# Sums kept in PSUM at the ends of two MLPs, rotary tables formed later, and a last pair of rows taken block by block, in a two-layer hybrid backbone

## The chip, the cores and the metric

The kernel runs on one core of a Trainium2 chip. The metric is device time in microseconds (us) of one execution, lower is better. The runs before the change give a median of 1191.76 us.

Names of engines in what follows: PE is the matrix engine, DVE the vector engine, ACT the scalar engine, POOL the gpsimd engine and SP the one that issues DMAs. PSUM is the accumulator memory that PE writes; ACT and DVE read and write it too.

## The reference, cut to what matters

A latent stream of 512 rows and a context stream of 256 rows, each row 1024 wide, go through two layers. Layer 0 mixes by pooling, layer 1 by attention (8 query heads, 2 key heads, width 128, rotary positions on latent rows), and each mixer is followed by a squared-ReLU MLP with 4096 hidden units. In layer 1 only the latent rows are needed behind the attention.

```python
def rms_norm(x, g):
    y = xf * lax.rsqrt(jnp.mean(xf * xf, axis=-1, keepdims=True) + EPS)
    return (y * g).astype(x.dtype)
def sq_relu_mlp(h, w_in, w_out):
    return jnp.square(jax.nn.relu(h @ w_in)) @ w_out
...
h_lat = modulate(rms_norm(x, g_mix_pre[i]), sh1, sc1)
...
x = x + gt1 * rms_norm(y_lat, g_mix_post[i])
m_lat = sq_relu_mlp(modulate(rms_norm(x, g_mlp_pre[i]), sh2, sc2), w_mlp_in[i], w_mlp_out[i])
x = x + gt2 * rms_norm(m_lat, g_mlp_post[i])
```

All is float32. Matrix products are made of three float32r products (high by high, high by low, low by high), so every operand is split into a rounded part "hi" (ACT) and a remainder "lo" (DVE).

## The kernel before, in words

Rows are handled in tiles of 128: latent tiles 0 to 3, context tiles 4 and 5. The stages follow one another: layer 0's mixer, layer 0's MLP (MLP0), keys, values and queries of layer 1 (K/V and Q), attention by head and tile, the attention's output product, layer 1's MLP (MLP1).

**The end of an MLP.** The hidden units are worked off in 16 groups of 256. The MLP's sums stand in `acc` in SBUF, one row of 1024 for each tile. `finish` does the last two groups: `out_mm` makes 24 matmuls for a tile into two PSUM tiles of 512 columns (three tiles of 512, 256 and 256 for the last tile of MLP1, `THIRDS`), and `out_ev` adds each to `acc` on DVE (L795). Then, per tile, `norm_a` squares the sum on ACT (L157, L158) and takes the power on POOL (L162), `norm_g` multiplies it by the gate on DVE (L321), `norm_r` adds it to the residual `xr` on DVE (L324), `norm_s` squares the new row (L157), and `norm_c` scales it into a row of `acc` (L496 on ACT or L498 on DVE). The tiles come in the order 4, 5, 0, 1, 2, 3. In the middle groups some tiles are "seeded": ACT copies `acc` into PSUM first (L775), PE adds on top, and ACT copies the sum back (L793).

**A pair of rows.** `modulated_pair` turns two finished rows: 16 transposes on PE (L349) into PSUM tiles `psx`, scale and shift of each 256-wide block (L357 on DVE or L360 on ACT, by a tuple), the hi split on ACT (L363 or L368) and the lo split on DVE (L364 or L369). In `fine` form the splits go by two blocks, else by four. The result feeds the next product on PE: K/V (L1028) behind MLP0, MLP1's first product (L566) behind the attention.

**Rotary tables.** `rope_load` fetches cosine and sine tables, `rope_tables` multiplies them by the head gains with six DVE instructions (L1013, L1017). `head_norm` reads them for latent tiles (L1053, L1056).

**The attention's output.** `attn_mm` makes the product (psy, L1269); `attn_ev` first multiplies by the gate on DVE (L321), then squares on ACT (L157). The last tile's second half comes as two pieces of 256. MLP1's first group is worked in two halves of 256 rows each, so that the first half can run while the last pair is prepared; its two hidden blocks f are worked one behind the other.

**What sets the order.** Each step is put at a hand-written time in `Steps`; a scheduler with a simulated timeline then orders every engine's instructions. Instructions marked `keep_in_program_order` stay in the order of the code. PSUM has two pools: `psA` (two tiles of two banks) and `psB` (four tiles of one bank: pso, psq, pk, psy and, for narrow pairs, psx).

Of the kernel before, what the change touches and what calls it, by code (L numbers as in the profile page):

```python
# [53 lines left out]
def backbone(ctx: ExitStack, tc, x, c, ctx_in, c_ctx, w_ada, b_ada, g_mix_pre, g_mix_post,  # L54
# [315 lines left out]

    gflat = gate.rearrange("p a n -> p (a n)")
# [121 lines left out]
    def norm_c(t, act, pool):  # L493
        r = rs[t][:, 0:1]
        if act:
            sc.activation(accv[:, t, :], xr[:, t, :], AF.Copy, scale=r)  # L496
        else:
            (gp if pool else ve).tensor_scalar(out=accv[:, t, :], in0=xr[:, t, :], scalar1=r, scalar2=None,  # L498
                                               op0=ALU.mult)
# [267 lines left out]
    def out_mm(i, parts, t, cols=HALVES):  # L767
        at_ = place_of[t] if i == 0 else t
        ts_ = slice(at_ * P, (at_ + 1) * P)
        seeded[t] = i == 0 and parts[0][0] > 0 and len(parts) == 1 and t in (1, 4) and stale[0] <= 0  # L770
        stale[0] -= 2
        pss = [psB.tile([P, 512], F32, tag="b", name="pso") for _ in cols]
        if seeded[t]:
            for (c0, w), ps in zip(cols, pss):
                sc.copy(ps, accv[:, t, c0:c0 + w])  # L775
# [11 lines left out]
    def out_ev(i, parts, t, cols=HALVES):  # L787
        for (c0, w), ps in zip(cols, pso[t]):
# [46 lines left out]
    def mlp1(inner, last):  # L835
# [38 lines left out]
        def squares(inner, q):  # L874
            for f in range(2):
                inner.part(len(inner.chunks) - 1, f)
# [133 lines left out]
    def rope_tables():  # L1010
        for w in (1, 0):
            g = grow[:, w, :]
            ve.tensor_tensor(out=tabs[:, w, 0], in0=tabs[:, w, 0],  # L1013
                             in1=g.unsqueeze(1).broadcast_to([P, NL, HD]), op=ALU.mult)
            for o in range(2):
                d = tabs[:, w, 1].rearrange("p t (h o d) -> p t h o d", o=2, d=32)[:, :, :, o, :]
                ve.tensor_tensor(out=d, in0=d, in1=swap(g, 1 - o).unsqueeze(1).broadcast_to([P, NL, 2, 32]),  # L1017
                                 op=ALU.mult)
# [49 lines left out]

    def norm_a(t, cols=HALVES):
        ss = sm_tile("ss")  # L1070
        for n, (c0, w) in enumerate(cols):
            mean_square(accv[:, t, c0:c0 + w], ss, n)
        rs[t] = rstd(ss, len(cols))

    def norm_g(t, pool=False, cols=HALVES):
        yg[t] = work_tile()
        for c0, w in cols:
            z = gated(t, yg[t], accv[:, t, c0:c0 + w], c0, c0 + w, pool)
            if cols == THIRDS:
                tc.keep_in_program_order(z)  # L1080
# [37 lines left out]
    def last0(st, n, t):  # L1118
        st.at([5.25, 10.45, 15.65, 20.85, 26.05, 31.25][n], norm_a, t)
        st.at([5.473, 10.6, 15.8, 21, 26.2, 31.4][n], norm_g, t, (False, False, False, False, False, False)[n])  # L1120
        st.at([8.8, 14, 19.2, 24.4, 29.6, 34.8][n], norm_r, t, (False, True, False, False, False, False)[n])
        st.at([10, 16.738, 20.4, 25.6, 30.8, 36][n], norm_s, t, (False, False, False, False, True, False)[n])
# [281 lines left out]
```

## Time and profile before

| | us |
|---|---|
| runs before: lowest, median, highest | 1187.81, 1191.76, 1194.09 |
| profiled execution, its own time | 1193.66 |
| its span | 1191.9 |
| PE busy | 1149.0 (96%) |
| DVE busy | 941.9 (79%) |
| ACT busy | 643.8 (54%) |
| POOL busy | 74.5 (6%) |

The profiled execution's own time is 1.76 us more than its span. Times in the views count from the span's start. A row of a timeline gives start, length, engine, line, operation, operands and count, and in brackets the idle time before it with what ended it; rows of one line that follow each other are merged, and a matmul's last piece overlaps the next row's start.

### The profile page before, as it was taken

Reading aid. Unit: us, or ns where it says so; the run is one execution under the profiler, and the core shown is the slowest. Engines: PE = TensorE matmul, PEld = TensorE weight load, DVE = VectorE, ACT = ScalarE, POOL = GpSimd, SP = SyncE. Lnnn points to the kernel's source line nnn. Section 1 sums busy time; section 2 is a strip of 40 time slices with the busy share of each in tenths; the row PEclk is TensorE's granted clock in tenths of the full one; section 3 lists DMA queues with packets and bytes.
Section 4 is the critical chain, followed back from the end, with each engine's and each line's share of the span. In section 5 each row is a group of like instructions: output and inputs, shape, how many; then the busy total and the mean of one; then the engine's idle time right before and its main releaser. Section 6 shows DMA issues by size and latency. Waiting matters only on the chain.

```text
span 1191.9 us, 15641 instructions
## 1 busy us (share of the span) xinstructions
PE 1149.0 (96%) x6026; PEld 993.8 (83%) x6026; DVE 941.9 (79%) x1521; ACT 643.8 (54%) x1141; POOL 74.5 (6%) x88
## 2 busy tenths in 40 slices
PE   6889999999999999999989989999899999999997
PEld 5568989899889888998867879998888888888886
DVE  5666686889989898998786589978677788778876
ACT  4676665445345534555775347872677346435523
POOL 1010000000000000000221232001000000000000
PEclk9899999999999999999998989999999999999999
DMA  9993222334434444344422111006244133314302
GB/s 339 389 319 121 72 75 102 118 130 142 157 126 142 141 140 144 107 155 138 166 71 79 64 36 37 1 6 207 108 140 145 39 135 123 113 47 142 106 31 111
DMA packets 92985, 147.88 MB, mean 124 GB/s; under 512 B 2752, under 2 KB 67824, under 8 KB 92912
## 3 DMA queue, kind: packets, MB, share of 16 engines
q1 hardware_dynamic: 92912, 146.90, 36.1%
q8 instruction: 47, 0.77, 0.3%
q14 instruction: 26, 0.21, 0.1%
HBM read 139.55 MB, written 7.34 MB: 123 GB/s over the span
## 4 chain that ended last, share of the span: by engine, by line
issue 45%; PE 43%; DVE 4%; ACT 3%; DMA 2%; POOL 2%; POOLq 0%; DVEq 0%; SPq 0%; ACTq 0%
PE psin L566 14%; PE pso L886 11%; PE psy L1269 3%; PE psq L1028 3%; PE po L1243 3%; PE pss L1204 2%; PE pspool L465 2%; PE pso L783 1%; PE pspt L1229 1%; ACT junk L157 1%; DMA raw<-in_w_ada 1%; POOL rs L162 1%; PE psada L229 1%; POOL rs L1037 1%; DVE work L321 1%
## 5 line engine op out<-in xcount | busy, mean ns | idle before, releaser
L783 PE MATMUL pso<-units,rb 128*128 128x512 f32 x1152 | 277.0, 392 | 0.0
L783 PEld LDWEIGHTS pso<-units,rb 128*128 128x128 f32 x1152 | 214.9, 188 | 41.7
L268 DVE SCALAR_TENSOR_TENSOR rows<-raw,cond,rows 128x256 f32<-128x256 f32 x280 | 123.0, 482 | 0.7
L795 DVE TENSOR_TENSOR acc<-acc,pso 128x512 f32<-128x512 f32 (+1 forms) x133 | 87.6, 675 | 34.5 <-PE pso L783 34.2
L566 PE MATMUL psin<-ra,rb 128*128 128x512 f32 (+2 forms) x384 | 103.2, 363 | 2.6 <-ACT ra L363 1.6
L162 POOL TENSOR_TENSOR rs<-ss,nhalf 128x1 f32<-128x1 f32 x42 | 27.1, 646 | 954.2 <-ACT ss L158 951.0
L886 PE MATMUL pso<-units,pairs 128*128 128x512 f32 x336 | 82.5, 389 | 0.0
L566 PEld LDWEIGHTS psin<-ra,rb 128*128 128x128 f32 x384 | 69.9, 192 | 13.1 <-ACT ra L535 1.9
L566 PE MATMUL psin<-ra 128*128 128x512 f32 x256 | 80.6, 389 | 0.0
L886 PEld LDWEIGHTS pso<-units,pairs 128*128 128x128 f32 x336 | 63.1, 188 | 13.1
L890 DVE TENSOR_TENSOR acc<-acc,pso 128x512 f32<-128x512 f32 x72 | 48.6, 681 | 29.0 <-PE pso L886 29.0
L677 PE MATMUL psin<-ra,units 128*128 128x384 f32 x336 | 65.7, 337 | 0.4 <-ACT psin L689 0.4
L677 PE MATMUL psin<-sums,units 128*128 128x384 f32 x336 | 63.6, 336 | 0.0
L677 PEld LDWEIGHTS psin<-ra,units 128*128 128x128 f32 x336 | 59.7, 188 | 3.1 <-ACT psin L689 0.5
L677 PEld LDWEIGHTS psin<-sums,units 128*128 128x128 f32 x336 | 59.0, 188 | 1.3
L566 PEld LDWEIGHTS psin<-ra 128*128 128x128 f32 x256 | 48.1, 188 | 10.0
L566 PE MATMUL psin<-rb 128*128 128x512 f32 (+1 forms) x144 | 53.5, 372 | 0.3 <-DVE rb L364 0.2
L1028 PE MATMUL psq<-units,ra 128*128 128x512 f32 x216 | 52.0, 393 | 0.0
L566 PE MATMUL psin<-rb,ra 128*128 128x512 f32 x128 | 49.8, 389 | 0.0
L122 DVE TENSOR_TENSOR units<-raw,units 128x1024 fp32r<-128x1024 f32 x34 | 41.2, 1216 | 9.7 <-ACT units L121 9.6
L1028 PEld LDWEIGHTS psq<-units,ra 128*128 128x128 f32 x216 | 40.1, 188 | 8.4 <-DVE ra L364 0.2
L793 ACT COPY acc<-pso 128x512 f32<-128x512 f32 x44 | 24.6, 586 | 35.8 <-PE pso L783 35.7
(271 smaller groups left out, 2379.8 us busy)
## 6 DMA issues: line engine op xcount, KB each, us to landing
raw<-in_w_ada SPq DMA_DIRECT2D x48, 1024.0 KB, 5.3
raw<-in_w_mlp_in SPq DMA_DIRECT2D x32, 1024.0 KB, 5.3
raw<-in_w_mlp_out SPq DMA_DIRECT2D x32, 1024.0 KB, 5.9
raw<-in_w_qkv SPq DMA_DIRECT2D x6, 1024.0 KB, 5.2
spill<-xr SPq DMA_DIRECT2D x10, 512.0 KB, 8.6
xr<-spill SPq DMA_DIRECT2D x10, 512.0 KB, 6.8
raw<-in_w_o SPq DMA_DIRECT2D x4, 1024.0 KB, 5.4
xr<-in_x SPq DMA_DIRECT2D x4, 512.0 KB, 4.9
```

The source lines that it names most:

```text
L122: ve.tensor_tensor(out=lo[:, z], in0=raw[:, z], in1=hi[:, z], op=ALU.subtract)):
L162: gp.tensor_tensor(out=r[:, 0:1], in0=ss[:, parts + 3:parts + 4], in1=nhalf[:, 0:1], op=ALU.pow)
L268: ve.scalar_tensor_tensor(out=r, in0=raw[:, k, :], scalar=cond[:, k, c:c + 1], in1=r, op0=ALU.mult, op1=ALU.add)
L566: te.matmul(ps[:, bank, o:o + ln], w[:, k, fs], a[:, k, t0:t0 + ln], start=(k == 0 and n == 0), stop=(k == KT - 1 and n == 2))
L677: te.matmul(bank, w[k], a[k], start=start and k == 0 and m == 0, stop=stop and k == 3 and m == 2, skip_group_check=True)
L783: te.matmul(pss[h][:, 0:cols[h][1]], a[:, f, ts_], w[:, f, cols[h][0]:sum(cols[h])], start=(n == 0 and not seeded[t]), stop=(n == len(seq) ...
L795: ve.tensor_tensor(out=d, in0=d, in1=ps[:, 0:w], op=ALU.add)
L886: te.matmul(ps, a, w, start=(m == 0), stop=(m == len(seq) - 1))
L890: ve.tensor_tensor(out=M[n][:, t], in0=M[n][:, t], in1=ps, op=ALU.add)
L1028: te.matmul(ps, a[:, k, sl], w[:, k % 4, :], start=(k == 0 and n == 0), stop=(k == KT - 1 and n == 2))
L1243: te.matmul(po[:, 0:256], v[:, kt, hs], p[:, kt, qs], start=(kt == 0 and n == 0), stop=(kt == NT - 1 and n == 2))
L1269: te.matmul(ps, a[:, k, sl], w[:, k % 4, o:o + width], start=(k == 0 and n == 0), stop=(k == KT - 1 and n == 2))
```

## The change

Four things change.

1. In `finish`, the sums of tiles 0 to 3 (MLP0) and of tiles 2 and 3 (MLP1) are seeded: ACT copies `acc` into the PSUM tile before the matmuls, PE adds on top, and `out_ev` does nothing for them. `norm_a` and `norm_g` then read the sum from PSUM (`summed`). Tiles 4 and 5 (MLP0), 0 and 1 (MLP1) stay as they were.
2. The steps of MLP0's last tiles get earlier times; tile 3's row is scaled on DVE; `rope_tables` moves from time 18.4 to 38.5, and its six instructions are kept in program order.
3. The attention's last pair gets a function of its own, `last_pair`: transposes of row tile 2 first and then those of row tile 3, all in `psB`, scale, hi and lo split block by block (256 wide). Tile 3's residual and squares are done in halves and its row is scaled half on DVE and half on ACT; tile 2's row is scaled on DVE; tile 3 is squared before it is gated.
4. MLP1's first group works the first four k blocks for both hidden blocks f before it goes on.

```diff
+    def last_pair(t, i, s, hi, lo, on_act):
+        works, sh = [accv[:, t + u, :] for u in range(2)], (SH1, SH2)[s] * KT
+        pss = [psB.tile([P, 2, 256], F32, tag="b", name="psx") for _ in range(KT // 2)]
+        for u in range(2):
+            for k in range(KT):
+                te.transpose(pss[k // 2][:, k % 2, u * P:(u + 1) * P], works[u][:, k * P:(k + 1) * P], ident)
+        for k in range(KT):
...
+            if on_act[k]:
+                sc.activation(h, src, AF.Identity, scale=sa, bias=b)
+            else:
+                ve.tensor_scalar(out=h, in0=src, scalar1=sa, scalar2=b, op0=ALU.mult, op1=ALU.add)
+            sc.copy(hi[:, k, z], h)
+            ve.tensor_tensor(out=lo[:, k, z], in0=h, in1=hi[:, k, z], op=ALU.subtract)
...
-    def norm_c(t, act, pool):
+    def norm_c(t, act, pool, half=False):
         r = rs[t][:, 0:1]
+        if half:
+            ve.tensor_scalar(out=accv[:, t, 0:512], in0=xr[:, t, 0:512], scalar1=r, scalar2=None, op0=ALU.mult)
+            sc.activation(accv[:, t, 512:D], xr[:, t, 512:D], AF.Copy, scale=r)
+            return
...
-        seeded[t] = i == 0 and parts[0][0] > 0 and len(parts) == 1 and t in (1, 4) and stale[0] <= 0
+        if len(parts) > 1:
+            seeded[t] = t not in ((4, 5), (0, 1))[i]
+        else:
+            seeded[t] = i == 0 and parts[0][0] > 0 and t in (1, 4) and stale[0] <= 0
...
     def out_ev(i, parts, t, cols=HALVES):
+        if len(parts) > 1 and seeded[t]:
+            return
...
+            n = len(inner.chunks) - 1
+            early_ = range(KT // 2 if n else 0)
+            for k in early_:
+                for f in range(2):
+                    inner.part(n, f, (k,))
             for f in range(2):
-                inner.part(len(inner.chunks) - 1, f)
+                inner.part(n, f, range(len(early_), KT))
...
+    def summed(t, cols):
+        return [ps[:, 0:w] if seeded[t] else accv[:, t, c0:c0 + w] for (c0, w), ps in zip(cols, pso[t])]
+
     def norm_a(t, cols=HALVES):
         ss = sm_tile("ss")
-        for n, (c0, w) in enumerate(cols):
-            mean_square(accv[:, t, c0:c0 + w], ss, n)
+        for n, src in enumerate(summed(t, cols)):
+            mean_square(src, ss, n)
...
-        st.at([10, 16.738, 20.4, 25.6, 30.8, 36][n], norm_s, t, (False, False, False, False, True, False)[n])
+        st.at([10, 16.738, 20.4, 25.6, 28.5, 30.4][n], norm_s, t, (False, False, False, False, True, False)[n])
...
-            st.at(18.4, rope_tables)
+            st.at(38.5, rope_tables)
...
+            last = (ch, t) == (1, NL - 1)
+            if last:
+                mean_square(ps, ss1[t], ch + n)
             gated(t, y1[:, t, :], ps, c0, c0 + width)
-            mean_square(ps, ss1[t], ch + n)
+            if not last:
+                mean_square(ps, ss1[t], ch + n)
...
+                if t == 3:
+                    at(47.4, last_pair, 2, 1, 1, h1H, h1L, (False, False, True, True, False, False, True, True))
```

How the order moves is read at three places; each row is a line, an operation, its output and inputs, the size and the count. The line numbers behind the change are those of the changed file.

On PE, where K/V begins behind MLP0's last product: `psx` are the transposes of the pairs (L349 in both files), `psq` the K/V products (L1028 before, L1061 now) and `pk` the transposed keys. Before:

```order
L1028 MATMUL psq<-units,ra 128x512 x10
L1028 MATMUL psq<-rb,ra 128x512 x2
L1028 MATMUL psq<-units,ra 128x512 x12
L1028 MATMUL psq<-rb,ra 128x512 x12
L1028 MATMUL psq<-units,ra 128x512 x12
L349 MATMUL psx<-ident,acc 128x128 x16
L1101 MATMUL pk<-ident,xr 128x128 x2
```

Now:

```order
L1061 MATMUL psq<-units,ra 128x512 x18
L349 MATMUL psx<-ident,acc 128x128
L1061 MATMUL psq<-rb,ra 128x512 x6
L349 MATMUL psx<-ident,acc 128x128
L1061 MATMUL psq<-rb,ra 128x512 x6
L1061 MATMUL psq<-units,ra 128x512 x8
L349 MATMUL psx<-ident,acc 128x128 x14
L1061 MATMUL psq<-units,ra 128x512 x4
L1135 MATMUL pk<-ident,xr 128x128 x2
```

Before, all 72 products of tiles 4, 5 and 0 stand ahead of the last pair's 16 transposes; now the pair's first transpose stands behind 48 of them, and its last 14 behind 68.

On ACT, in MLP0's last product: L157 and L158 square a sum (`acc`, now `pso`) or a row (`xr`), L496 (now L517) scales a finished row, L799 is the seeding copy. Before:

```order
L157 ACTIVATE junk,ss<-acc 128x512
L496 ACTIVATE acc<-xr,rs 128x1024
L158 ACTIVATE ss<-ss,phase 128x1
L157 ACTIVATE junk,ss<-acc 128x512
L158 ACTIVATE ss<-ss 128x1
L157 ACTIVATE junk,ss<-xr 128x1024
L158 ACTIVATE ss<-ss,phase 128x1
```

Now:

```order
L157 ACTIVATE junk,ss<-pso 128x512
L517 ACTIVATE acc<-xr,rs 128x1024
L799 COPY pso<-acc 128x512
L158 ACTIVATE ss<-ss 128x1
L799 COPY pso<-acc 128x512
L157 ACTIVATE junk,ss<-xr 128x1024
L158 ACTIVATE ss<-ss,phase 128x1
```

The two seeding copies of tile 2 stand behind the scaled row of tile 4, which waits for POOL; PE's matmuls of tile 2 wait for these copies. Tile 3's copies stand likewise behind the scaled row of tile 0.

On DVE, at the attention's last pair: L369 is the lo split of the pair of tiles 0 and 1, L324 the residual of tile 3, L498 (now L519) and L513 scale rows, L357 and L384 scale and shift transposed blocks, L364 and L386 are lo splits. Before:

```order
L369 TENSOR_TENSOR rb<-acc,ra 128x4x256
L324 SCALAR_TENSOR_TENSOR xr<-acc,rs,xr 128x1024
L498 TENSOR_SCALAR acc<-xr,rs 128x1024
L357 TENSOR_SCALAR acc<-psx,avec_97,mods_93 128x256 x4
L364 TENSOR_TENSOR rb<-acc,ra 128x2x256 x4
L132 TENSOR_TENSOR ra<-raw,ra 128x2048
```

Now:

```order
L324 SCALAR_TENSOR_TENSOR xr<-acc,rs,xr 128x512
L369 TENSOR_TENSOR rb<-acc,ra 128x4x256
L324 SCALAR_TENSOR_TENSOR xr<-acc,rs,xr 128x512
L513 TENSOR_SCALAR acc<-xr,rs 128x512
L384 TENSOR_SCALAR acc<-psx,avec_97,mods_93 128x256 x4
L386 TENSOR_TENSOR rb<-acc,ra 128x256 x8
L132 TENSOR_TENSOR ra<-raw,ra 128x2048
```

The residual is halved around the lo split of the earlier pair, half of the row's scaling is left to ACT, and four wide lo splits become eight narrow ones.

40 lines of the change are left out of this document (21 added, 19 removed).

## The prediction

> **What bounds the kernel now.** I read the page's first part, then the table of windows around the three places that the change touches, then the timeline of each engine there. The busy times of the engines:
>
> ```profile
> PE 1149.0 (96%) x6026; PEld 993.8 (83%) x6026; DVE 941.9 (79%) x1521; ACT 643.8 (54%) x1141; POOL 74.5 (6%) x88
> ```
>
> PE is busy in 1149.0 of 1191.9 us. Since the change takes no matmul away, all that can be won is PE's idle time, the time it ran at half clock, and what lies behind its last matmul; work taken from DVE or ACT counts only where PE waits for them. The windows at these places (columns: window, length, busy PE, PEld, DVE, ACT, POOL, granted clock, DMA share, GB/s):
>
> ```profile
> 567.00:603.00 36.00, 36.00 (x170) 29.97 (x169) 26.12 (x34) 25.51 (x55) 11.66 (x11) 1.00 0.34 128
> 599.30:621.20 21.90, 20.74 (x96) 15.95 (x95) 20.00 (x33) 16.64 (x41) 7.12 (x7) 1.00 0.31 97
> 622.51:625.93 3.42, 1.24 (x7) 0.80 (x5) 1.57 (x2) 2.30 (x8) 0.54 (x1) 1.00 0.00 0
> 625.93:632.76 6.83, 5.30 (x21) 4.92 (x22) 4.54 (x12) 4.91 (x15) 2.75 (x7) 0.50 0.01 2
> 640.00:700.00 60.00, 59.56 (x277) 49.55 (x277) 40.91 (x69) 27.12 (x93) 15.98 (x23) 1.00 0.22 71
> 851.21:854.62 3.41, 1.65 (x14) 1.45 (x14) 0.75 (x1) 1.32 (x4) 0.55 (x1) 1.00 0.39 154
> 854.62:858.03 3.41, 1.55 (x12) 1.11 (x11) 2.82 (x6) 3.41 (x7) 0.00 (x0) 1.00 0.01 2
> 858.03:861.45 3.42, 3.42 (x17) 3.42 (x18) 2.56 (x4) 3.41 (x4) 0.00 (x0) 0.50 0.00 0
> 860.50:890.80 30.30, 30.30 (x150) 25.87 (x149) 26.41 (x26) 21.07 (x30) 0.00 (x0) 0.98 0.40 139
> ```
>
> MLP0's end (567 to 603) has PE busy throughout. Behind it K/V loses time in two ways, by waits and by a clock of 0.50 from 625.93 to 632.76. The same pair of losses stands at the attention's last pair (851 to 861). So the change can gain at these two places and at the end of the program, and lose in 567 to 603, where nothing is to be won.
>
> **The change, term A: MLP0's end to K/V.** PE's timeline there:
>
> ```profile
> 595.45 1.69 PE L349 MATMUL psx<-ident,acc 128*128 128x128 f32 x14
> 596.89 6.16 PE L783 MATMUL pso<-units,rb 128*128 128x512 f32 x26
> ...
> 617.64 3.16 PE L1028 MATMUL psq<-rb,ra 128*128 128x512 f32 x10 [0.81 <-DVE ra L364]
> 620.63 2.90 PE L1028 MATMUL psq<-units,ra 128*128 128x512 f32 x12
> 623.37 0.38 PE L349 MATMUL psx<-ident,acc 128*128 128x128 f32 x2
> 627.46 3.25 PE L349 MATMUL psx<-ident,acc 128*128 128x128 f32 x14 [3.71 <-ACT acc L496]
> ```
>
> From the starts, a K/V product costs (623.37 - 620.63)/12 = 0.228 and a transpose (596.89 - 595.45)/14 = 0.103. MLP0's last product starts ahead of 602.9. The 72 products and 32 transposes behind it need 72 x 0.228 + 32 x 0.103 = 19.7, so without a wait they would end at 622.6. They end at 627.46 + 3.25 = 630.7: 8.1 lost. The greatest part is the wait of 3.71 for tile 3's scaled row (L496), the next the half clock, at which the 14 transposes take 3.25 in place of 1.45 (1.8 lost). The rest of the half-clock stretch to 632.76 costs (632.76 - 630.7)/2 = 1.0 more. So 9.1 is the most that can be had.
>
> What ACT does there, and tile 3's chain:
>
> ```profile
> 598.97 1.06 ACT L157 ACTIVATE junk<-xr 128x1024 bf16<-128x1024 f32 x1 [1.59 <-DVE xr L324]
> 619.45 0.62 ACT L157 ACTIVATE junk<-acc 128x512 bf16<-128x512 f32 x1
> 622.37 1.28 DVE L324 SCALAR_TENSOR_TENSOR xr<-work,rs,xr 128x1024 f32<-128x1024 f32 x1 [0.46 <-POOL rs L162]
> 626.27 1.14 ACT L496 ACTIVATE acc<-xr,rs 128x1024 f32<-128x1024 f32 x1
> ```
>
> Tile 3's sum is squared only at 619.45, 17 us behind its product. Now the squares read PSUM and their steps come earlier. By the order, what ACT has from the square at 598.97 to tile 2's scaled row is: seven casts of 512 (0.52 from start to start), four blocks of L360 (0.47), six squares of 512 with their reads (0.62), seven L158 (0.2), two squares of 1024 and two scaled rows (1.05 each): 14.9 together. Without idle time the row is ready at 613.9; I add half of the idle time that ACT had there before (599.3 to 621.2: 21.90 - 16.64 = 5.26), since L360 still waits for transposes: 616.5. PE, with 48 products and 16 transposes behind it, is there at 602.9 + 12.6 = 615.5. The next products take a hi (a cast, 617.1) and a lo of 0.7 on DVE (617.8). Tile 3's row follows: by the order its last L158 has two casts, two L360, a cast and a small cast ahead of it, about 3.5 us, then POOL 0.55 and DVE's scaling 0.75, so 621.4 against 627.4 before. PE, with 18 products and 2 transposes behind 617.8, reaches its 14 transposes at 622.1: the long wait is gone. 22 products and 16 transposes from 617.8 take 6.7, end 624.5; with 1.5 for short waits, as much as before, 626.0. Gain 630.7 - 626.0 = 4.7, and 1.0 for the half clock behind it.
>
> Against it stand the rotary tables:
>
> ```profile
> 610.00 0.68 DVE L1013 TENSOR_TENSOR acc<-acc,grow 128x512 f32<-128x512 f32 x1
> 610.60 0.74 DVE L1017 TENSOR_TENSOR acc<-acc,grow 128x256 f32<-128x256 f32 x2
> ```
>
> Twice this is 2.8 us, formerly in DVE's gaps, now between tile 3's row and the last pair's scaling (L357) on DVE. K/V products of the last pair wait for these blocks, and the first rotary use follows. Bounds 0 and 2.8; I take 0.7, a quarter, as ACT takes some of the eight blocks and products of the earlier pairs stand between. **A = -4.7 - 1.0 + 0.7 = -5.0**. Bounds: -0.3 (ACT as idle as before, 2.6 later, and the tables at 2.8) and -7.5 (ACT with no idle time, so that PE's own 615.5 counts, 1.0 more, and no short waits, 1.5 more).
>
> The seeds are costed at nothing. The relevant rows:
>
> ```profile
> L775 ACT COPY pso<-acc 128x512 f32<-128x512 f32 x44 | 25.6, 587 | 27.0 <-DVE acc L795 26.9
> 579.81 4.69 POOL L132 TENSOR_TENSOR rb<-raw,rb 128x2048 fp32r<-128x2048 f32 x1 [1.25 <-ACT rb L129]
> 586.91 1.14 ACT L496 ACTIVATE acc<-xr,rs 128x1024 f32<-128x1024 f32 x1
> 595.61 1.14 ACT L496 ACTIVATE acc<-xr,rs 128x1024 f32<-128x1024 f32 x1
> ```
>
> Thirteen copies at 0.587 (three of them shorter) are 7.2 us on ACT, eight of them in 567 to 603, where ACT is busy 25.51 of 36; 25.5 + 4.7 = 30.2 still fits. But PE waits for each. A tile's 24 products take 24 x 0.228 = 5.5: back from 602.9 PE wants tile 3's seed at 597.4, and, with 16 transposes more, tile 2's at 590.2. Tile 2's copies follow tile 4's row (586.91 + 1.14 = 588.05): 588.6 and 589.4. Tile 3's follow tile 0's row (596.75 at its old time): 597.3, and the second at 598.0, wanted at 600.1. The order has a tile's first half ahead of its second, so it fits by 1.6 us at tile 2 and by 0.1 at tile 3; the old time of tile 0's row is a late one, as two squares that waited for L795 stood ahead of it. If the cover fails, the rival below gives the price. The thirteen evictions that DVE loses (0.675 each, 8.8 us) free time where PE didn't wait for DVE, save in term C.
>
> **Term B: the attention's last pair.**
>
> ```profile
> 847.96 0.38 ACT L157 ACTIVATE junk<-psy 128x256 bf16<-128x256 f32 x1
> 849.75 1.29 DVE L324 SCALAR_TENSOR_TENSOR xr<-acc,rs,xr 128x1024 f32<-128x1024 f32 x1 [0.44 <-POOL rs L162]
> 853.21 0.75 DVE L498 TENSOR_SCALAR acc<-xr,rs 128x1024 f32<-128x1024 f32 x1 [2.17 <-POOL rs L162]
> 854.02 1.53 PE L349 MATMUL psx<-ident,acc 128*128 128x128 f32 x12 [1.76 <-DVE acc L498]
> 857.19 0.50 PE L566 MATMUL psin<-ra,rb 128*128 128x256 f32 x2 [1.64 <-ACT ra L363]
> 857.91 0.49 PE L566 MATMUL psin<-rb 128*128 128x256 f32 x1 [0.22 <-DVE rb L364]
> 857.17 2.50 DVE L364 TENSOR_TENSOR rb<-acc,ra 128x512 fp32r<-128x512 f32 x4
> 860.52 2.29 DVE L132 TENSOR_TENSOR ra<-raw,ra 128x2048 fp32r<-128x2048 f32 x1 [0.86 <-ACT ra L129]
> 865.01 0.40 PE L566 MATMUL psin<-ra 128*128 128x512 f32 x1
> ```
>
> Tile 3's row is ready at 853.96. The square of its last piece no longer waits for the gate (before, at 847.96, it stood behind a 1024 cast), the residual of 1.29 and the square overlap by halves, and the scaling of 0.75 is shared by two engines: I take 1.7 for all three, row at 852.3. Tile 2's transposes are then done, so eight remain (0.8), and scale, hi and lo of one block, by half of the 512-wide rows some 0.5, 0.35 and 0.4, with the starts between: first product at 854.3, the first with a lo at 855.0 (before 857.2 and 857.9). 48 narrow products at 0.121 end at 860.9, where before they end at 865.0 with 1.7 lost to the half clock. That is 4.1 earlier. The next weights limit it: their lo (L132) ends at 862.8 before and moves only with DVE, whose pieces grow from four of 0.64 to eight of 0.42, so I put the small end at 0.9, the wait ahead of L132 that ACT's cast made; and DVE is busy 26.41 of the 30.30 us behind. The weights of the first groups are, however, there for another k, so I stand nearer the upper end: **B = -3.0**, bounds -0.9 and -4.1.
>
> On the clock: the windows 851.21 to 854.62 and 854.62 to 858.03 had PE busy 1.65 and 1.55 of 3.41, neither of them idle, and the next one got 0.50. By that row a half-busy window is enough. Now the first window would hold about 2.1 busy and the second about 3, which lie above it, so full clock is assumed. [...]
>
> **Term C: the end.**
>
> ```profile
> 1185.00 0.42 DVE L795 TENSOR_TENSOR acc<-acc,pso 128x256 f32<-128x256 f32 x1 [0.55 <-PE pso L783]
> 1185.84 0.40 ACT L157 ACTIVATE junk<-acc 128x256 bf16<-128x256 f32 x1
> 1186.80 0.55 POOL L162 TENSOR_TENSOR rs<-ss,nhalf 128x1 f32<-128x1 f32 x1 [4.72 <-ACT ss L158]
> 1187.38 1.42 DVE L324 SCALAR_TENSOR_TENSOR xr<-work,rs,xr 128x512 f32<-128x512 f32 x2 [0.69 <-POOL rs L162]
> ```
>
> The last piece no longer passes L795 (0.42). Its square began at 1185.84, another 0.42 behind the eviction's end, as it stood behind the square of the piece before; that one is rid of its eviction too. **C = -0.8**, bounds -0.4 (ACT's queue stays) and -0.84 (all of both). The power on POOL and L324 stay as they are, and the seeds of MLP1 stand well ahead of them.
>
> MLP1's interleaved f blocks only make room for B and are counted there.
>
> **The sum.** -5.0 - 3.0 - 0.8 = -8.8. Against the profiled execution's own 1193.66 that is 1184.9; it lies 1.9 above the median of the runs, so on 1191.76 the forecast is **1183.0**.
>
> **The rivals.**
>
> *Seeds late (slower).* ACT is in order: if tile 4's row waits for POOL beyond 589.6, or tile 0's beyond 596.8, PE stops with nothing else to run. The 4.69 us on POOL at 579.81 is such a stretch, and the powers stand behind it in POOL's queue. With 3 us at each of two tiles and a half clock for 10.2 us (three windows, 5.1 lost) it costs 11.1, and with ACT late A's gain is gone: -3.8 + 11.1 = +7.3, 1199.1. Against it: powers now start earlier, by the evictions left out.
>
> *A is absorbed (same).* If Q and what follows start by DVE or POOL, a K/V that ends 5 us sooner only waits later; -3.8, 1188.0. For it: the rotary tables are pushed towards Q. Against it: PE is busy 59.56 of 60 in 640 to 700, DVE 40.91.
>
> *B stays behind the weights (small gain).* B = -0.9: sum -6.7, 1185.1. For it: L132 waited for ACT's cast of these weights before (0.86 ahead of 860.52), and that cast stays behind the pair's eight hi splits.
>
> *It does not do what it says:* the order shows the evictions gone and rows earlier; only waits can undo it. 1191.8.
>
> **How the numbers follow.** About 0.5% (6 us) is what a measurement of this kernel can tell from no change: faster is under 1185.8. Forecast 0.56, B behind the weights 0.12, A absorbed 0.20, seeds late 0.09, nothing gained 0.03. Faster takes 0.54 of the first and 0.07 of the second: 0.61; slower is 0.09; the rest 0.30. Low: all upper bounds are -7.5 - 4.1 - 0.8 = -12.4, 1179.4, less 1.4 for the scatter of the runs, 1178.0. High: the small ends give -0.3 - 0.9 - 0.4 = -1.6, 1190.2, plus 0.8 for the same scatter, 1191.0; the late seeds and no gain lie outside.
>
> **What would show it.** Right: PE's wait of 3.71 ahead of the 14 transposes is gone and 625.93 to 632.76 is at full clock; L807's matmuls (the former L783) have no idle time before tiles 2 and 3; the first wide product of MLP1 some 3 us earlier from the pair's start; L795 absent behind the last matmul. Wrong: idle time of PE ended by the seeding copy, a DVE that is still the releaser of K/V's products behind the rotary tables, or a Q stage that starts no earlier.

## The result and the profile after

| | before | changed |
|---|---|---|
| median of the runs, us (4 each) | 1192.69 | 1183.24 |
| lowest and highest | 1187.81, 1194.09 | 1180.60, 1184.12 |
| span of the profiled execution | 1191.9 | 1178.8 |

The ratio of the times is 0.9924, 95% interval 0.9903 to 0.9946: faster by 9.4 us, where 8.8 was forecast (1183.0).

PE, DVE, ACT and POOL in the changed kernel, and the windows at the two places (window, length, busy PE, PEld, DVE, ACT, POOL, granted clock, DMA share, GB/s):

```profile
PE 1145.2 (97%) x6026; PEld 989.4 (84%) x6026; DVE 935.4 (79%) x1515; ACT 648.6 (55%) x1160; POOL 75.9 (6%) x88
```

```profile
566.50:602.20 35.70, 35.67 (x166) 29.37 (x164) 24.55 (x29) 28.94 (x63) 12.53 (x10) 1.00 0.34 123
602.20:622.80 20.60, 20.53 (x106) 16.79 (x106) 16.05 (x27) 17.13 (x46) 8.53 (x12) 1.00 0.31 102
624.98:631.80 6.82, 6.82 (x32) 5.46 (x31) 6.19 (x14) 4.38 (x14) 0.89 (x2) 1.00 0.00 0
842.70:846.15 3.45, 2.20 (x13) 1.36 (x11) 2.90 (x8) 3.45 (x10) 0.00 (x0) 1.00 0.00 0
846.15:849.56 3.41, 3.41 (x17) 3.41 (x18) 2.21 (x6) 3.41 (x5) 0.00 (x0) 0.51 0.01 2
```

Through MLP0's last product (566 to 602) PE is still not idle (35.67 of 35.70), so no seed is late; through K/V (602 to 623) it is hardly idle either (20.53 of 20.60), and the half clock is gone there. At the last pair a half clock of 3.41 us stays. The first seeding copies of tiles 2 and 3, and the matmuls that need them:

```profile
586.99 0.58 ACT L799 COPY pso<-acc 128x512 f32<-128x512 f32 x1
589.35 5.73 PE L807 MATMUL pso<-units,rb 128*128 128x512 f32 x24
...
595.17 0.59 ACT L799 COPY pso<-acc 128x512 f32<-128x512 f32 x1
596.36 5.70 PE L807 MATMUL pso<-units,rb 128*128 128x512 f32 x24
```

The copies end at 587.57 and 595.76, 1.8 and 0.6 us ahead of PE.

PE's timeline of the changed kernel where the 3.71 stood, and the row that it had waited for on DVE, with ACT's row of tile 2:

```profile
618.36 2.00 PE L1061 MATMUL psq<-units,ra 128*128 128x512 f32 x8
620.20 1.69 PE L349 MATMUL psx<-ident,acc 128*128 128x128 f32 x14
621.65 1.17 PE L1061 MATMUL psq<-units,ra 128*128 128x512 f32 x4
...
612.94 1.15 ACT L517 ACTIVATE acc<-xr,rs 128x1024 f32<-128x1024 f32 x1
...
617.85 0.75 DVE L519 TENSOR_SCALAR acc<-xr,rs 128x1024 f32<-128x1024 f32 x1
```

Tile 3's row is there at 618.6, 1.6 ahead of its transposes; the 14 take 1.69 where they took 3.25.

At the last pair, PE and the end of the program:

```profile
841.99 1.09 PE L376 MATMUL psx<-ident,acc 128*128 128x128 f32 x8
844.05 0.50 PE L587 MATMUL psin<-ra,rb 128*128 128x256 f32 x2 [0.97 <-ACT ra L385]
844.76 0.39 PE L587 MATMUL psin<-rb 128*128 128x256 f32 x1 [0.20 <-DVE rb L386]
852.70 0.50 PE L587 MATMUL psin<-ra 128*128 128x512 f32 x1
...
1171.87 0.88 PE L807 MATMUL pso<-units 128*128 128x256 f32 x6
1172.79 0.38 ACT L157 ACTIVATE junk<-pso 128x256 bf16<-128x256 f32 x1 [0.63 <-PE pso L807]
1174.32 1.41 DVE L324 SCALAR_TENSOR_TENSOR xr<-work,rs,xr 128x512 f32<-128x512 f32 x2 [0.60 <-POOL rs L162]
```

One wait of 0.97 is left of 1.76 and 1.64. At the end the square starts straight behind PE (1172.79), with no eviction between, and the last residual 1.57 behind PE's end at 1172.75; before it was 1187.38 - 1184.96 = 2.42 (its last six matmuls: 1184.08, 0.88).

**Where the 13.1 us between the two profiled spans lie.** PE has 6026 matmuls in both, so the start of the one with the same number can be compared at any place at which the order is alike again. To the 3,100th (MLP0's last product) the changed kernel is 1.0 us ahead: scatter of the beginning, where nothing differs. So a time on the changed trace's clock is 1.0 less than the same moment on the clock of before, up to there. From there to the 3,400th (the first queries) it gains 7.85: term A. To the 3,700th (start of the attention) 1.4 more: behind the same wait (3.50 and 3.51) the half clock lasts 10.24 us in the one trace (704.43 to 714.67, granted 0.50) and 6.83 in the other (696.01 to 702.84, granted 0.50). From the 4,480th to the 4,600th (the last pair) 1.95: term B. Behind the last matmul 0.85: term C. A, B and C make 10.65. The same numbers are given for the experiments below, against the changed kernel's trace: "A +1.1" says that this stretch was 1.1 us longer there.

### The profile page after: what moved, and what is told of

Read it like the earlier page. It is cut to its first block, busy times and chain, and to the rows that moved or that the text cites. A ratio compares the mean times of both kernels' runs of the same rounds, so it can differ in the third digit from the quotient of the medians.

```text
span 1178.8 us, 15653 instructions
## 1 busy us (share of the span) xinstructions
PE 1145.2 (97%) x6026; PEld 989.4 (84%) x6026; DVE 935.4 (79%) x1515; ACT 648.6 (55%) x1160; POOL 75.9 (6%) x88
## 4 chain that ended last, share of the span: by engine, by line
PE 82%; issue 5%; ACT 5%; DVE 4%; POOL 2%; DMA 1%; POOLq 0%; DVEq 0%; SPq 0%; ACTq 0%
PE pso L807 22%; PE psin L698 18%; PE psin L587 17%; PE pso L917 11%; PE psy L1303 4%; PE po L1277 3%; PE pss L1238 2%; PE pspool L482 1%; ACT junk L157 1%; PE pspt L1263 1%; POOL rs L1070 1%; PE psada L229 1%; POOL rs L162 1%; DVE work L1086 1%; ACT ss L158 1%
## 5 line engine op out<-in xcount | busy, mean ns | idle before, releaser
L821 DVE TENSOR_TENSOR acc<-acc,pso 128x512 f32<-128x512 f32 x120 | 79.6, 679 | 32.3 <-PE pso L807 32.2
L917 PEld LDWEIGHTS pso<-units,pairs 128*128 128x128 f32 x336 | 63.1, 188 | 13.1
L921 DVE TENSOR_TENSOR acc<-acc,pso 128x512 f32<-128x512 f32 x72 | 48.7, 682 | 28.5 <-PE pso L917 28.5
L1061 PE MATMUL psq<-units,ra 128*128 128x512 f32 x216 | 52.1, 392 | 0.0
L799 ACT COPY pso<-acc 128x512 f32<-128x512 f32 (+1 forms) x57 | 32.6, 578 | 26.9 <-DVE acc L821 26.7
L1061 PEld LDWEIGHTS psq<-units,ra 128*128 128x128 f32 x216 | 40.1, 188 | 8.2
```

What stands on the lines that cost most here:

```text
L821: ve.tensor_tensor(out=d, in0=d, in1=ps[:, 0:w], op=ALU.add)
L917: te.matmul(ps, a, w, start=(m == 0), stop=(m == len(seq) - 1))
L921: ve.tensor_tensor(out=M[n][:, t], in0=M[n][:, t], in1=ps, op=ALU.add)
L1061: te.matmul(ps, a[:, k, sl], w[:, k % 4, :], start=(k == 0 and n == 0), stop=(k == KT - 1 and n == 2))
```

## The experiments

Eleven more kernels were run, eight of them the changed kernel with a part of the change taken back or altered; ratios are to the kernel before. Runs of one kernel differ by 0.3% and more, so a difference under 3 us is read in the traces: by the ratios, only the two runs at 0.9974 and 0.9967 can be told from the changed kernel's 0.9924.

**No seeds in MLP0.**

```diff
-            seeded[t] = t not in ((4, 5), (0, 1))[i]
+            seeded[t] = i == 1 and t not in (0, 1)
```

> The changed kernel, but MLP0's tiles 0 to 3 are not seeded: the evictions L821 (formerly L795) are back for them and the squares read acc; all step times stay as changed. In the traces of before and after, the K/V products behind MLP0 end 7.9 us earlier once the different start of the two executions (1.0) is taken off. Theory (the forecast's reason: tile 3's row comes early because its squares no longer stand behind evictions and late steps, and both the seeds and the times matter): eviction puts tile 3's squares some 2 us later, its row at about 620.5 in place of 618.6 on the after trace's clock, so K/V ends 0.5 to 2 us later than after, and 1 more where a half clock comes back; total +1 to +3 us against after. Rival S (the seeds carry the gain): the wait of 3 to 4 us ahead of the last 14 transposes returns, +7 to +8. Rival T (the step times alone carry it, seeds are worth nothing): 0 within 0.5 us in the trace.

Ratio 0.9974 (0.9954 to 0.9993). The earlier step times put tile 3's squares and gate ahead of its own evictions, so they read the sum without the last product; the time is that of such a kernel. A +6.7. DVE's rows show what it did: tile 3's two evictions are done only behind its scaled row.

```profile
622.19 0.74 DVE L519 TENSOR_SCALAR acc<-xr,rs 128x1024 f32<-128x1024 f32 x1
623.53 0.42 DVE L1077 TENSOR_TENSOR work<-psq,rs 128x256 f32<-128x256 f32 x1 [0.60 <-POOL rs L1070]
623.88 1.27 DVE L821 TENSOR_TENSOR acc<-acc,pso 128x512 f32<-128x512 f32 x2
```

The two PSUM tiles stay taken until 625. It doesn't tell the theories apart; the run after the next has the same edit with the evictions ahead.

**Seeds, but the old times.** The rows of `last0` are those of before, tile 3's row on ACT:

```diff
-        st.at([5.25, 10.45, 15.65, 20.85, 26.05, 27][n], norm_a, t)
+        st.at([5.25, 10.45, 15.65, 20.85, 26.05, 31.25][n], norm_a, t)
...
-        st.at([12, 17.906, 22.4, 27.6, 30.2, 30.6][n], norm_c, t, (True, True, True, True, True, False)[n], (False, False, False, False, False, False)[n])
+        st.at([12, 17.906, 22.4, 27.6, 32.8, 36.716][n], norm_c, t, (True, True, True, True, True, True)[n], (False, False, False, False, False, False)[n])
```

> The changed kernel with the five rows of MLP0's last steps as before (tile 3's norm steps at their old times, its row scaled on ACT); the seeds stay, and the rotary tables stay late. Theory (both matter): without the earlier times ACT does tile 3's squares and row behind other work again, tile 3's row comes at 623 to 625 on the after trace's clock in place of 618.6, the wait ahead of the last 14 transposes is 2 to 4 us, total +3 to +6 us against after. Rival T (times carry it all): +7 to +8. Rival S (seeds carry it all): 0 to +1.

Ratio 0.9931 (0.9907 to 0.9955), median 1181.34. A +1.1: only a short wait is back.

```profile
625.08 1.75 PE L349 MATMUL psx<-ident,acc 128*128 128x128 f32 x14 [0.83 <-ACT acc L517]
```

The theory (+3 to +6) missed. The seeds without the earlier times bring almost all of A.

**No seeds in MLP0, evictions ahead.** As the first, and tile 3's evictions ahead of its squares:

```diff
-            st.at(5.2 * n + 5.2, out_ev, i, parts, t, cols)
+            st.at(26.98 if (i, n) == (0, 5) else 5.2 * n + 5.2, out_ev, i, parts, t, cols)
```

> The changed kernel without the seeds of MLP0's tiles 0 to 3, and with tile 3's eviction put ahead of its squares, so that everything is computed as before; the earlier step times stay. The run with the old times and the seeds kept lost only 1.1 us of the 7.8 between the start of MLP0's last product and the K/V products behind it. Theory (changed by that run: the seeds carry nearly all of term A, since squares from PSUM spare ACT the wait for DVE's evictions, and the times alone little): K/V end +4 to +7 against after in the trace, PE waiting for tile 3's row or for a hi or lo split of an earlier pair. The forecast's reading (times and seeds both): +1 to +3. Rival (either of the two alone is enough, since the first 1.6 us of earliness are slack): 0 to +1.

Ratio 0.9937 (0.9917 to 0.9957), median 1182.06. A +2.3. Without any seed in MLP0 the long wait is gone too, and 16 transposes follow the products without idle time:

```profile
616.81 2.89 PE L1061 MATMUL psq<-units,ra 128*128 128x512 f32 x12
619.53 2.19 PE L349 MATMUL psx<-ident,acc 128*128 128x128 f32 x16
...
629.52 2.55 PE L1061 MATMUL psq<-rb,ra 128*128 128x512 f32 x10 [0.74 <-DVE ra L369]
```

ACT's squares wait 0.65 and 0.75 for evictions there, and short waits for splits make up the 2.3. The theory of the moment, that the seeds carry the gain (+4 to +7), fell. The 2.3 lies in the range given for the forecast's reading, that seeds and times both matter (+1 to +3); the rival, that either alone is enough (0 to +1), is right about the long wait, but not about the short ones.

**Neither.** Both edits together; the late tables, the new pair and MLP1's seeds stay.

```diff
-            seeded[t] = t not in ((4, 5), (0, 1))[i]
+            seeded[t] = i == 1 and t not in (0, 1)
...
-        st.at([5.25, 10.45, 15.65, 20.85, 26.05, 27][n], norm_a, t)
+        st.at([5.25, 10.45, 15.65, 20.85, 26.05, 31.25][n], norm_a, t)
```

> The changed kernel without the seeds of MLP0's tiles 0 to 3 and with the old times of its last steps; the rotary tables stay late, the new pair and MLP1's seeds stay. From the start of MLP0's last product to the K/V products behind it, before takes 7.8 us more than after; with the seeds alone (old times) it is 1.1 more, with the times alone (no seeds) 2.3 more. Theory (each of the two alone takes most of it, since either brings tile 3's row ahead of the moment PE asks for it; they are not additive): without both, 6.5 to 8.5 more, with the wait of about 3.7 for tile 3's row ahead of the last 14 transposes and a half clock in most executions. Rival (additive: 1.1 + 2.3, the rest is the late rotary tables): 3 to 4.5.

Ratio 0.9967 (0.9949 to 0.9985), median 1187.73. A +7.55, as the theory had it, and the wait is back with the half clock (14 transposes in 3.25):

```profile
624.23 3.25 PE L349 MATMUL psx<-ident,acc 128*128 128x128 f32 x14 [4.77 <-ACT acc L517]
```

So A belongs to the seeds and to the times, and not additively: 1.1 is lost without the one, 2.3 without the other, 7.55 without both. The tables moved late, the only part of A's edits left here, bring no more than the remaining 0.3.

**Rotary tables at their old time.**

```diff
-            st.at(38.5, rope_tables)
+            st.at(18.4, rope_tables)
```

> The changed kernel with the rotary tables back at time 18.4 (still in program order). The forecast put 0.7 us against the change for moving them later. In the after trace they run at 620.87 to 623.5 on DVE, and PE has no idle time from 602.2 to 640. Theory now: moving them costs nothing, since K/V's products behind were covered; back in their old place they stand ahead of tile 2's and 3's residuals on DVE, 0 to 2 us of which reach tile 3's row, and PE has 1.6 us in hand there (row 618.6, transposes at 620.2): total 0, within 0.5 in the trace. The forecast's term: -0.7 (early tables are better). Rival (the late tables are what frees DVE and so carry the gain): +2 or more with a wait ahead of the last transposes.

Ratio 0.9930 (0.9905 to 0.9955), median 1181.68. A +0.9, by one wait for a lo split, behind which table rows and the scalings stand on DVE:

```profile
616.66 1.20 PE L1061 MATMUL psq<-rb,ra 128*128 128x512 f32 x4 [0.88 <-DVE ra L364]
```

```profile
613.29 0.69 DVE L1044 TENSOR_TENSOR acc<-acc,grow 128x512 f32<-128x512 f32 x1
613.89 0.75 DVE L1049 TENSOR_TENSOR acc<-acc,grow 128x256 f32<-128x256 f32 x2
614.56 1.44 DVE L357 TENSOR_SCALAR acc<-psx,avec,mods 128x256 f32<-128x256 f32 x3
615.92 0.68 DVE L364 TENSOR_TENSOR ra<-acc,ra 128x512 fp32r<-128x512 f32 x1
```

Late is 0.9 better, where the forecast had it 0.7 worse, and the theory of this run had 0 within 0.5: the sign of that term was wrong, with the rest of the change in place.

**Seeds of tiles 2 and 3 made three times.**

```diff
-                sc.copy(ps[:, 0:w], accv[:, t, c0:c0 + w])
+                for _ in range(3 if i == 0 and len(parts) > 1 and t in (2, 3) else 1):
+                    sc.copy(ps[:, 0:w], accv[:, t, c0:c0 + w])
```

> The changed kernel with each seeding copy of MLP0's tiles 2 and 3 made three times (the same values), eight copies more on ACT, 0.52 from start to start: 4.2 us. It doubles and more the cost that the forecast put at nothing. On the after trace, tile 2's copies end 1.8 us ahead of PE's need and tile 3's first one 0.6 ahead (595.76 against 596.36). Theory (the seeds are covered, but by little): tile 3's first half is about 0.5 to 1.5 us late, PE shows that idle time ahead of tile 3's product, and the chain of tile 3's row behind it comes 2 to 4 us later, of which PE has 1.6 in hand: total +1.5 to +4 against after. Rival (ACT's work there is on PE's path one for one): +4.2. Rival (ACT has room for all): 0 to +0.5, no idle time of PE.

Ratio 0.9939 (0.9914 to 0.9963), median 1183.36. A and MLP0's product together +3.4. PE now waits for both tiles' seeds:

```profile
589.93 5.74 PE L808 MATMUL pso<-units,rb 128*128 128x512 f32 x24 [1.33 <-ACT pso L800]
598.67 5.74 PE L808 MATMUL pso<-units,rb 128*128 128x512 f32 x24 [1.47 <-ACT pso L800]
```

The copies that PE waits for are the last of these rows of ACT:

```profile
588.79 1.09 ACT L800 COPY pso<-acc 128x512 f32<-128x512 f32 x2
...
597.52 1.09 ACT L800 COPY pso<-acc 128x512 f32<-128x512 f32 x2
```

They end at 589.88 and 598.61 on this trace's clock, which shows the same moment 1.0 earlier than the changed kernel's: 3.3 and 3.8 us later than the first copies there (587.57 and 595.76). At the same matmul PE is 1.6 late at tile 2 and 3.3 at tile 3, so 1.7 and 0.5 us were in hand, near the margins that had been read (1.8 and 0.6). The theory held; what is hidden at tile 3 is hidden by half a microsecond.

**The attention's last pair as before.** The old function, residual, square and row of tile 3 whole, tile 2's row on ACT, and gate ahead of square (two of the edits shown):

```diff
-                    at(47.4, last_pair, 2, 1, 1, h1H, h1L, (False, False, True, True, False, False, True, True))
+                    at(47.4, norm_pair, 2, 1, 1, h1H, h1L, False, True, (True, False, True, False, True, False, True, False))
...
-            last = (ch, t) == (1, NL - 1)
+            last = False
```

> The changed kernel with the attention's last pair as before (the old pair function with its tuple, the row of tile 3 on DVE whole, tile 2's row on ACT, residual and square whole, gate ahead of square); MLP1's interleaved f blocks stay. The two traces differ there by 2.0 us (12.2 earlier behind the pair, 10.25 ahead of it), where the sum had 3.0 and the half clock of 3.4 us behind the pair's wait stayed. Theory: +2.0 us against after in the trace, the same half-clock window behind the pair. Rival (the interleaved f blocks give that gain, not the pair's function): 0 to +0.5. Rival (the granted clock is what differs): the trace shows a second half-clock window and +3.7.

Ratio 0.9920 (0.9895 to 0.9944), median 1180.85. PE's waits are those of before:

```profile
843.42 1.53 PE L349 MATMUL psx<-ident,acc 128*128 128x128 f32 x12 [1.77 <-DVE acc L519]
846.58 0.50 PE L587 MATMUL psin<-ra,rb 128*128 128x256 f32 x2 [1.63 <-ACT ra L363]
```

Yet B is only +0.57, for the half clock doesn't come here:

```profile
839.53:842.94 3.41, 2.12 (x18) 1.92 (x16) 1.24 (x2) 1.44 (x3) 0.55 (x1) 1.00 0.41 157
842.94:846.35 3.41, 1.53 (x12) 1.29 (x12) 2.17 (x5) 2.35 (x5) 0.00 (x0) 1.00 0.00 1
846.35:849.76 3.41, 2.95 (x22) 2.75 (x23) 2.71 (x5) 3.41 (x5) 0.00 (x0) 1.00 0.00 0
```

The run with the old times has the new pair and no half clock either; its B is -1.49 (at a granted 0.50 a half clock of 3.41 can lose 1.7 at most). Between these two, alike in clock, the pair's edit is worth 0.57 + 1.49 = 2.06; between before and after, both with a half clock, 1.95. That is B at a like clock, whole, so little or nothing is left for the interleaved f blocks, which this run kept. Less than about 0.35 can't be told: by that much B differs between the changed kernel and the run without MLP0's seeds, evictions ahead, both with the new pair and a half clock. The theory's +2.0 with the half clock in place did not come; it holds only at a like clock.

**No seeds in MLP1.**

```diff
-            seeded[t] = t not in ((4, 5), (0, 1))[i]
+            seeded[t] = i == 0 and t not in (4, 5)
```

> The changed kernel without the seeds of MLP1's tiles 2 and 3: evictions are back, squares read acc. Theory (term C): +0.85 us in the trace between PE's last matmul and the end, none before it; from the last matmul's end (1184.96 before, 1172.75 after) to the last residual's start 1.57 after, 2.42 here as before. Rival (the gain came from the reordering of the last pieces on ACT and is kept): under +0.4.

One profiled execution. The end is as before, the last residual 1174.19 - 1171.76 = 2.43 behind PE's end (the last six matmuls: 1170.88, 0.88):

```profile
1172.10 0.42 DVE L821 TENSOR_TENSOR acc<-acc,pso 128x256 f32<-128x256 f32 x1
1172.56 0.43 DVE L321 TENSOR_TENSOR work<-acc,gate 128x256 f32<-128x256 f32 x1
1174.19 1.41 DVE L324 SCALAR_TENSOR_TENSOR xr<-work,rs,xr 128x512 f32<-128x512 f32 x2 [1.21 <-POOL rs L162]
```

Term C is 2.43 - 1.57 = 0.86, all by the seeds.

**The pair's wait filled.** Eight matmuls of data that are ready, into PSUM that the real product overwrites:

```diff
+            if n:
+                inner.part(n, 0, ())
+                (wH, _), (aH, _) = inner.w, inner.a
+                for _ in range(8):
+                    tc.keep_in_program_order(te.matmul(inner.ps[0][:, 1, 0:256], wH[:, 0, 0:P], aH[:, 0, 0:256],
+                                                       start=True, stop=True))
```

(The last eight transposes are kept in program order with them.)

> The changed kernel with eight matmuls of 256 columns put between the attention's last eight transposes and the first product that waits for them; they read data that are ready and write a PSUM region that the real product overwrites. They take 0.86 us of PE's wait of 0.97. The after trace has clock 0.50 from 846.15 to 849.56 behind this wait; the traces of the runs with old times and with the old pair have none there, though both have such a wait, and the old pair a longer one. Theory (the half clock comes where the wait falls in a certain way on the clock's own time grid): here too it is there or not by the grid, the pair's stretch +-0.2 where the granted clock is alike, and 1.7 less where there is no half clock. Rival (the granted clock follows what PE has done in the window before, and the filled wait prevents it): no half clock behind the pair, -1.7 in the trace there. One execution without half clock does not by itself tell these apart; one with it refutes the rival.

Ratio 0.9910 (0.9884 to 0.9935), median 1179.23. B -1.5, no half clock; the eight matmuls take 1.22 up to the next one's start (844.17 to 845.39), where 0.86 was the author's estimate:

```profile
843.33 1.09 PE L376 MATMUL psx<-ident,acc 128*128 128x128 f32 x8
844.17 1.19 PE L909 MATMUL psin<-ra,rb 128*128 128x256 f32 x8
845.39 0.50 PE L589 MATMUL psin<-ra,rb 128*128 128x256 f32 x2
```

The eight profiled executions that have the new pair and no filling split evenly: four have the half clock behind it (the changed kernel, the early tables, both runs with MLP0's seeds off and the new times), four have none (old times, thrice seeded, no seeds in MLP1, neither). The three filled ones have none. None of three against four of eight doesn't settle that the filling does it.

The traces say more about the four and four. Within a trace the half clocks begin whole multiples of 3.413 us apart (in the changed kernel at 696.01 and 846.20, 44 of them; in the trace of before at 625.93, 704.43 and 858.03, 23 and 45 of them). Taking this for a grid, the moments at which one could begin can be reckoned. In the four executions with a half clock such a moment lies 3.1 to 3.4 us behind the end of the pair's last transposes (846.20 - 843.08 = 3.12 in the changed kernel); in the four without, it lies 1.35 to 1.4 behind (three) or 0.8 (one). The theory of a time grid fits all eight, though this was read off afterwards. In the three filled ones the moment lies 3.1, 3.5 and 1.4 behind: two of them were within 0.2 us of where the unfilled pair got its half clock, and had none. That speaks for the filling, without showing it.

**The first split of the attention's output weights off POOL**, on top of the filled wait; whole on DVE, or in quarters at later times:

```diff
-        at(7.01, lambda: split(*raws[0], True, True, True))
+        at(7.01, lambda: split(*raws[0], False, True, False))
...
-        at(11.396, lambda: split(*raws[1], True, True, True))
+        at(11.396, lambda: split(*raws[1], False, True, False))
```

> The kernel with the filled wait, and also: the first two splits of the attention's output weights make their lo part on DVE instead of POOL. In the after trace POOL's one lo split takes 4.71 us from 690.86, and two DVE instructions of 128x256 beside it take 5.62 together, where such instructions take 0.2 to 0.5 elsewhere; PE waits 3.5 us behind them at the start of the attention and gets a half clock for 6.8 us. Theory: on DVE the split costs 2.28 once and nothing stands still beside it; PE's wait at the attention's start shrinks by 2 to 3.5, the half clock goes in part: -3 to -5 us against the filled kernel, 1175. Rival (DVE's 2.28 stands in the same chain): -1 to 0. Rival (the lo split on DVE delays the softmax of the first steps): +1 to +2.

Ratio 0.9899 (0.9858 to 0.9941), median 1178.02, the lowest of all, though its interval holds the filled kernel's ratio. Against that kernel's trace the attention's beginning is 1.0 shorter, not 3 to 5. DVE before the split was moved and after:

```profile
691.31 5.52 DVE L1094 TENSOR_TENSOR work<-work,acc 128x256 f32<-128x256 f32 x2
696.75 0.54 DVE L1274 TENSOR_TENSOR units<-pspt,units 128x384 fp32r<-128x384 f32 x1
```

```profile
690.46 2.27 DVE L132 TENSOR_TENSOR ra<-raw,ra 128x2048 fp32r<-128x2048 f32 x1
692.65 0.55 DVE L1274 TENSOR_TENSOR units<-pspt,units 128x384 fp32r<-128x384 f32 x1
```

The standstill of 5.5 is gone, but 2.27 stands in the same place and PE still waits, 1.52 in place of 3.41; the rival had it. The half clock there went from 6.83 to 3.41 us, as expected in part, but PE's next wait for ACT's exponential (L1251) grew from 0.59 to 1.50.

```diff
-        at(7.01, lambda: split(*raws[0], True, True, True))
+        for q in range(4):
+            at((9.01, 9.51, 10.01, 10.51)[q], lambda q: split(*raws[0], False, True, False, q), q)
```

> As the run before, with both splits in quarters (512 wide: cast on POOL, lo on DVE at 0.6 each) at later times, so that they lie between the steps of the attention. Theory: as there, and no block of 2.28 ahead of the first softmax: -3.5 to -6 us against the filled kernel. Rival (what holds PE at the attention's start is not the split but the last query head's rotation): 0 to -1.

(The second split likewise, from 13.01.) Ratio 0.9897 (0.9858 to 0.9936), median 1178.94; 1.3 shorter there than the filled kernel, and again short of what was expected, if a little more than the rival's 0 to -1: the first scores are 4.1 earlier at the 3,600th matmul, and all but 1.3 of it is gone by the 3,900th. There is no half clock at the attention's start any more and no long wait of PE for DVE; in its place PE waits five times for ACT's steps of the softmax (L1251, L1261), 0.81 to 1.91 each and 5.4 together. ACT in turn waits for DVE's steps of it (L1250, L1257), and DVE is busy in all of the 12.00 us from 690: with the split out of the way, DVE's whole work there is what is left.

## Why the prediction was right, and where its steps were not

**The bound** held: PE was the path, and all gains lie where it waited, ran at half clock, or was through.

**Term A** was mis-sized: 5.0 forecast, 7.85 in the traces, a little beyond the upper bound of 7.5. The step that failed is what the sum added for waits, three terms. The first is ACT's idle time, half of the 5.26 of before: it put tile 2's row 17.5 us behind the square from which the sum was counted (598.97 to 616.5), 14.9 without idle time. In the changed trace it is 16.1 (598.02 to 614.09), early enough for PE's own 615.5 to count, so 1.0 was too much. The second, 1.5 for short waits, did not come (PE was busy 20.53 of 20.60). The third, 0.7 for the tables, was 0.9 the other way. Without the three the sum is 8.2; the bound of 7.5 still held the 0.7 for the tables, though their own bound was 0. The mechanism was right, but its cause was told as one chain, squares from PSUM and earlier steps together. The runs show two causes, either of which brings tile 3's row nearly in time; the forecast would not have told that from an edit with one of them.

**The seeds at nothing** was right: tile 3's first copy ended 0.6 us ahead of PE's need, where the text had 0.1. On the clock of before it ended at 596.7, not at 597.3, as tile 0's row came 0.5 earlier with its squares, the reason that the text gave. The rival of late seeds did not come, but the thrice-made copies show that its mechanism is real and that at tile 3 it decides from about 0.5 us on.

**Term B** was 3.0 and measured 1.95 to 2.06 at a like clock. Row 1.5 earlier (1.7 forecast), first product 2.9 earlier (2.9): these steps held. The step that failed is the clock, an estimate from one row: "the first window would hold about 2.1 busy ... which lie above it, so full clock is assumed". The window held 2.20 of 3.45, and the next one was granted 0.51, by which some 1.7 was lost again in this execution (3.41 us at 0.51). Where the half clock stays away behind the new pair alone, B is 1.95 + 1.5 = 3.45. The weights, to which the cut from 4.1 to 3.0 was put down, held nobody: the wide products follow at 852.70, 0.1 behind the narrow ones. Without the half clock they come close to it: with the old times their lo (L132) ends at 856.91, and the wide products start at 856.94.

On the clock, the reading that was taken from that row of before holds neither way. Half busy was to be enough for a half clock: with the old pair, 1.53 of 3.41 busy was followed by 1.00 (1.58 in the stretch of the clock's own grid, 843.22 to 846.63). More than half was to be safe: here 2.20 of 3.45 busy was followed by 0.51. The half clocks behind the wait at the attention's start begin at different points of the same instructions: 0.80 ahead of the next matmul in the trace of before (704.43 and 705.23), 0.37 ahead in the changed kernel's (696.01 and 696.38). What decides on a half clock, and how late it takes effect, stays open.

**Term C**: 0.8 forecast, 0.86 measured.

**The rivals**: A was not absorbed; all of it is still there at the 3,600th matmul, as PE is busy throughout the Q stage (50.00 of 50.00 us from 640). B was not held by the weights. **The sum**, 8.8 against 9.4 by the medians and 10.65 in two traces, came out near because A was under- and B over-sized; the two errors, +2.85 and -1.05, partly cancel, and the granted clock moves an execution by 1.4 at the attention's start and 1.5 at the pair. That the median came within 0.3 us of 1183.0 is luck.

## What to carry to other kernels

Where PE waits once for the end of a long chain on other engines, several unlike edits can each remove that wait, and their gains do not add (here 1.1 and 2.3 lost without one, 7.55 without both); try each alone before keeping all. Adding an accumulator into PSUM by a copy ahead of the product takes an eviction out of the chain behind it (0.42 at the end of MLP1), but puts a copy ahead of it (0.58 for 128x512), and how much later that copy may come is to be measured by making it longer. When two executions are compared, compare the same matmul in both, stage by stage, and set half-clock stretches apart before a stage's gain is put down to an edit.

## What the hardware showed that was not expected

The same pair of rows with the same wait of 0.97 got a half clock of 3.41 us in four profiled executions and none in four, worth 1.5 us; a wait of 3.4 to 3.5 at the attention's start got 6.83 in some and 10.24 in others, worth up to 1.5. The two go together: the four of these eight with 6.83 are the four that have the half clock at the pair, and the four with 10.24 have none there. So one of the two losses, the longer half clock here or the one at the pair, was always paid with the new pair, and they nearly cancel between executions. With the old pair it was both in the trace of before and neither in the run with the old pair. Of the 13.1 between the spans of before and after, 1.4 come from this and from no edit.

Two DVE instructions of 128x256 took 5.62 us (0.82 and 4.87; most other TENSOR_TENSOR of that size take 0.40 to 0.43) beside POOL's subtraction of 128x2048 (4.71 us) in the changed kernel:

```profile
690.23 5.62 DVE L1086 TENSOR_TENSOR work<-work,acc 128x256 f32<-128x256 f32 x2
690.86 4.71 POOL L132 TENSOR_TENSOR ra<-raw,ra 128x2048 fp32r<-128x2048 f32 x1
```

The second one ends at 695.85, 0.28 behind POOL's end. With the split moved to DVE the two (L1094) took 0.75 in place of 5.52, so the standstill was gone, yet only 1.0 us of it was left at the attention's beginning. What held the second one up beside POOL is not shown.
